# Hybrid decoder block on one core: squares of x one slot earlier, x fetched in two-k-tile rows on one queue, first slots multiplied by k-tile

## The chip, the core and the metric

The kernel runs on one NeuronCore of a Trainium2 chip. The metric is device time in microseconds (us), the median of three runs. Engines are named as the profile names them: PE is TensorE (PEld its weight loads), DVE is VectorE, ACT is ScalarE, POOL is GpSimd, SP is SyncE, which here issues most DMAs.

## What is computed

One decoder layer for 256 tokens and a model width of 1024, all in float32. Only the front of it matters here: an RMS norm whose result is multiplied by one wide weight matrix.

```python
n = rmsnorm(h, norm1_g[l])
z = n @ w_in[l]
cu, cg, q, k, v, gc, ga = jnp.split(z, cuts, axis=-1)
y_conv = conformer_conv(cu, cg, ...)
att = moba_attention(q, k, v, ...)
merged = sigmoid(gc) * y_conv + sigmoid(ga) * (att @ w_attn_out[l])
h = h + merged @ w_out[l]
h = h + swiglu(rmsnorm(h, norm2_g[l]), w_ffn_gate[l], w_ffn_up[l], w_ffn_down[l])
```

## The kernel before, in words

Every product is made of three float32r matmuls: each operand is split into a high part (rounded) and a low part (what the rounding left), and the product is high by high, low by high and high by low (L173 to L175 in `mm3`).

The weights come as a stream of **slots**. A slot is 512 KB: two k-tiles (128 rows of the matrix each) of 512 columns. For each slot a DMA fills a raw buffer (`stream_dma`, L137), ACT casts it to the high part `whi` (L154), DVE subtracts to get the low part `wlo` (L155; from slot 12 on POOL does every second one), and PE multiplies: 12 matmuls per slot, which are 2 token tiles by 2 k-tiles by 3. The first three slots are fetched and split in two pieces, one per k-tile. There are 5 raw buffers and 8 pairs of split buffers; the split runs 6 slots ahead of the multiplication. A slot's raw buffer is fetched anew when its low part has been made.

The first eight chunks of columns need `x`, transposed, as the stationary operand. `xT` holds the norm's gain in its first 16 columns and then eight k-tiles of 256 tokens. Five DMAs load it between the pieces of the first slots: k-tile 0 with the gain, k-tile 1, and then pairs (`load_x`, `between`). ACT makes the high part `xgh` (L698) and DVE the low part `xgl` (L699) of each k-tile, in `split_x`.

The norm's scale is not applied to `x`: the products are scaled when they leave PSUM. So the sum of squares is needed only after the first chunk (four slots). ACT squares `x` two k-tiles at a time (`square`, L709 and L712), POOL adds the four results up (three additions of 128x512, L713, and a last one of 128x256, L715), and four matmuls with one column (`ss`, L727, in `first_norm`) add up over the partitions. `first_norm` stands in `post[4]`, right behind slot 4 in PE's order. From `ss`, DVE and POOL make `rstd` (L728, L729), ACT's sigmoids `csg` (L318) and DVE's gating `ca` (L319) free the first chunk's PSUM banks and feed the convolution. That runs as 31 taps per channel tile on DVE (L271, L273), from transposed copies in PSUM that PE writes (`refill`, L261), while PE goes on with the slots.

The order of each engine's work is the order of the code. In a loop over six slots, before PE's loop, the code does the split of a slot, `split_x` of the next two k-tiles and one `square`:

```python
for i in range(6):
    stream_split(i + 1)
    for k in (2 * i + 2, 2 * i + 3):
        if k < KD:
            split_x(k)
    if i >= 2:
        square(i - 2)
```

In PE's loop a slot is multiplied for token tile 0 (`mm3(c, slot, g, 0)`), then come the DMA and split of later slots and the jobs of that slot, then token tile 1. Ten bf16 matmuls on a tile of zeros (L211) stand ahead of slot 0.

Of the kernel before, what the change touches and what calls it, by code (L numbers as in the profile page):

```python
# [19 lines left out]
T = S // P  # L20
# [5 lines left out]
CW = 512  # L26
G = 2
# [60 lines left out]
def hybrid_block(ctx: ExitStack, tc: tile.TileContext, x, xT, par, w_in, w_co, w_ao, w_o, w_gu, w_dn, out):  # L88
    nc = tc.nc
# [10 lines left out]
    def bank(name, *shape):  # L100
        return ps.tile([P, *shape], F32, tag="tr", bufs=2, name=name)


    slots = []
# [15 lines left out]
    raw, hi, lo = {}, {}, {}  # L120
    at = {"dma": 0, "split": 0}

    def shape_of(i):
        return (U, P) if isinstance(slots[i][0], Cols) else (G, CW)

    def parts(i):
        return [slice(j, j + 1) for j in range(G)] if i < 3 else [slice(None)]

    def stream_dma(upto):
        while at["dma"] < min(upto, len(slots)):  # L130
            i = at["dma"]
            c, g = slots[i]
            raw[i] = wp.tile([P, *shape_of(i)], F32, tag="raw", bufs=RAW_BUFS, name=f"raw{i}")
            for part in parts(i):
                if i == 0:
                    load_x(part.start, part.stop)
                (nc.sync if i or part.start else nc.scalar).dma_start(raw[i][:, part, :], c.w[g][:, part, :])  # L137
                between(i, part)
            at["dma"] += 1

# [3 lines left out]
    def stream_split(upto):  # L144
        while at["split"] < min(upto, len(slots)):
            i = at["split"]
            hi[i] = wp.tile([P, *shape_of(i)], F32R, tag="whi", bufs=SPL_BUFS, name=f"whi{i}")
            lo[i] = wp.tile([P, *shape_of(i)], F32R, tag="wlo", bufs=SPL_BUFS, name=f"wlo{i}")
            r = raw.pop(i)
            eng = nc.gpsimd if on_pool(i) else nc.vector  # L150
            for part in parts(i):
                if i == 0:
                    split_x(part.start)
                nc.scalar.copy(hi[i][:, part, :], r[:, part, :])  # L154
                eng.tensor_sub(lo[i][:, part, :], r[:, part, :], hi[i][:, part, :].bitcast(F32))  # L155
            at["split"] += 1
# [5 lines left out]
            .rearrange("p (k s) -> p k s", s=S) for x in "hl"  # L162
        )

    def mm3(c, i, g, t, acc=None, cols=slice(0, CW), first=0, last=None):

        xh, xl = c.lhs()
        acc = c.acc[t] if acc is None else acc
        last = c.nk - 1 if last is None else last
        tok = slice(t * P, (t + 1) * P)  # L170
        for j in range(G):
            k = g * G + j
            nc.tensor.matmul(acc, xh[:, k, tok], hi[i][:, j, cols], start=(k == first), stop=False)  # L173
            nc.tensor.matmul(acc, xl[:, k, tok], hi[i][:, j, cols], start=False, stop=False)  # L174
            nc.tensor.matmul(acc, xh[:, k, tok], lo[i][:, j, cols], start=False, stop=(k == last))  # L175
# [3 lines left out]
    def mm_cols(c, i, g, units, slot):  # L179
        xh, xl = c.rhs()  # L180
        for u in units:
            n, k = c.order[g * U + u]
            c.seen[n] += 1
            first, last = c.seen[n] == 1, c.seen[n] == c.nk
            if first:
                tag = GU_BANKS[banks["n"] % len(GU_BANKS)]
                banks["n"] += 1
                c.acc[n] = ps.tile([P, S], F32, tag=tag, bufs=4 if tag == "mm" else 1, name=f"{c.name}{n}")
            acc = c.acc[n]
            nc.tensor.matmul(acc, hi[i][:, u, :], xh[:, k, :], start=first, stop=False)  # L190
            nc.tensor.matmul(acc, hi[i][:, u, :], xl[:, k, :], start=False, stop=False)  # L191
            nc.tensor.matmul(acc, lo[i][:, u, :], xh[:, k, :], start=False, stop=last)  # L192
            if last:
                c.done(slot, n, c.acc.pop(n))
# [453 lines left out]
    def store(b, t, acc, cols=slice(0, CW)):  # L648
        to = slice(b * CW + cols.start, b * CW + cols.stop)
        o = sm.tile([P, cols.stop - cols.start], F32, tag="u", name=f"o{b}{t}{cols.start}")  # L650
        nc.vector.scalar_tensor_tensor(o, acc, rstd2[:, t : t + 1], xs[:, t, to], op0=ALU.mult, op1=ALU.add)
        nc.sync.dma_start(out[t * P : (t + 1) * P, to], o)
# [29 lines left out]
    def xk(k0, k1):  # L682
        return xt[:, XG + k0 * S : XG + k1 * S].rearrange("p (k s) -> p k s", s=S)

    def load_x(k0, k1):
        cols = slice(XG + k0 * S if k0 else 0, XG + k1 * S)
        nc.sync.dma_start(xt[:, cols], xT[:, cols])

    def between(i, part):
        if i == 0:  # L690
            if part.stop == G:
                load_x(2, 4)
        elif i < KD // 2 - 1 and part.stop == G:
            load_x(2 * i + 2, 2 * i + 4)

    def split_x(k):
        g, one = xt[:, k : k + 1], slice(k, k + 1)
        nc.scalar.activation(xg[0][0][:, one, :], xk(k, k + 1), AF.Copy, scale=g)  # L698
        nc.vector.scalar_tensor_tensor(xg[0][1][:, one, :], xk(k, k + 1), g, xg[0][0][:, one, :].bitcast(F32),  # L699
                                       op0=ALU.mult, op1=ALU.subtract)  # L700
# [5 lines left out]
    def square(q):  # L706

        if q == 0:
            nc.scalar.activation(sq, xk(0, 2), AF.Square)  # L709
            return  # L710
        s = sm.tile([P, 2, S], F32, tag="u", name=f"xsq{q}")
        nc.scalar.activation(s, xk(2 * q, 2 * q + 2), AF.Square)  # L712
        nc.gpsimd.tensor_add(sq, sq, s)  # L713
        if q == KD // 2 - 1:
            nc.gpsimd.tensor_add(sq[:, 0, :], sq[:, 0, :], sq[:, 1, :])  # L715

    for i in range(6):
        stream_split(i + 1)
        for k in (2 * i + 2, 2 * i + 3):
            if k < KD:  # L720
                split_x(k)
        if i >= 2:
            square(i - 2)
    def first_norm():
        ss = bank("ss", T)
        for t in range(T):
            nc.tensor.matmul(ss[:, t : t + 1], sq[:, 0, t * P : (t + 1) * P], ones, start=True, stop=True)  # L727
        nc.vector.tensor_scalar(rstd, ss, 1.0 / D, EPS, op0=ALU.mult, op1=ALU.add)  # L728
        nc.gpsimd.tensor_tensor(rstd, rstd, mhalf[:, :T], op=ALU.pow)  # L729
        nc.gpsimd.tensor_scalar_mul(rhalf, rstd, 0.5)  # L730
        nc.gpsimd.tensor_scalar_mul(gqs, prm[:, C_QG : C_QG + 1], float(P) ** -0.5)
# [7 lines left out]
    n = len(slots)  # L739
    tail = 3  # L740
    split_k = KF - tail * G
    for slot, (c, g) in enumerate(slots):
        rows = isinstance(c, Chunk)
        for job in pre.pop(slot, ()):
            job()
        if not rows:
            mm_cols(c, slot, g, range(U // 2), slot)
        elif g == 0:
            c.acc = [ps.tile([P, CW], F32, tag="mm", bufs=4, name=f"{c.name}_{t}") for t in range(T)]
        if rows and slot < n - tail:  # L750
            mm3(c, slot, g, 0)
        stream_dma(slot + AHEAD + RAW_BUFS)
        stream_split(slot + AHEAD)
        for job in jobs.pop(slot, ()):
            job()
        if not rows:
            mm_cols(c, slot, g, range(U // 2, U), slot)
        elif slot < n - tail:
            mm3(c, slot, g, 1, last=split_k - 1 if c is slots[-1][0] else None)
            if slot == n - tail - 1:  # L760
                end = xs[:, 1, D - CW :]
                nc.vector.scalar_tensor_tensor(end, c.acc[1], rstd2[:, 1:2], end, op0=ALU.mult, op1=ALU.add)
            for job in post.pop(slot, ()):
                job()
        elif slot == n - 1:
            for i in range(tail):
                mm3(c, n - tail + i, g - tail + 1 + i, 0)
            store(1, 0, c.acc[0])
            for part in range(2):
                cols = slice(part * CW // 2, (part + 1) * CW // 2)  # L770
                end = bank(f"end{part}", CW // 2)
                for i in range(tail):
                    mm3(c, n - tail + i, g - tail + 1 + i, 1, end, cols, first=split_k)
                store(1, 1, end, cols)
        load["pe"] += SLOT + pe_side.get(slot, 0.0)
        load["dve"] = max(load["dve"], load["pe"] - SLOT) + (0.0 if on_pool(slot + AHEAD) else LOW_PART) + dve_side.get(slot, 0.0)
        for job in late.pop(slot, ()):
            job()
        run_taps(slot, load["pe"] + LAG)
        if rows and g == c.nk // G - 1:  # L780
            c.done(slot, c.acc)
# [56 lines left out]
```

## Time and profile before

| what | value |
|---|---|
| median of 3 runs | 440.75 us (440.18 to 441.38) |
| the profiled execution | 441.83 us |
| its span, first to last instruction | 440.0 us |
| mean granted TensorE clock in the span | 0.996 of full |
| PE busy | 433.4 us (98%) |
| DVE, ACT, POOL busy | 316.7, 247.8, 90.1 us |

The page gives busy time by engine and the chain of work that ended last. The trace behind it answers with timelines of an engine (start, duration, engine, line, operation, tiles, and in brackets the idle time before it and what ended that), with waits in total, and with windows. A timeline merges neighbouring instructions of one line into a row with a count. A matmul's duration in a row is longer than its distance to the next, since matmuls overlap: distances are read from the starts.

### The profile page before, as it was taken

The page shows a single profiled execution, that of the slowest core. Times are in us where ns is not written, and L with a number is a line of the kernel's source. Part 1 is how long each engine was busy: PE and PEld are TensorE (multiplying, and loading weights), DVE is VectorE, ACT ScalarE, POOL GpSimd, SP SyncE. Part 2 cuts the span into 40 slices and gives each one's busy share as a digit, 9 for nine tenths or more (in the row PEclk, how much of TensorE's full clock was granted, in tenths as well). Part 3 has the DMA queues.
Part 4 walks back from the last instruction along what each step waited for, and adds up shares of the span by engine and source line. Part 5 has one row for each costly group of instructions (what it writes and reads, how often), then busy time and mean ns, then how long its engine had stood idle before and what let it go on. Part 6 is the DMA issues. An engine that isn't in the chain of part 4 may idle for free.

```text
span 440.0 us, 6863 instructions
## 1 busy us (share of the span) xinstructions
PE 433.4 (98%) x2514; PEld 378.1 (86%) x2514; DVE 316.7 (72%) x558; ACT 247.8 (56%) x451; POOL 90.1 (20%) x74
## 2 busy tenths in 40 slices
PE   8899999999999999999999999999999999999996
PEld 4678888888888888888888899999999999888886
DVE  4989998998889799967759368666666666744501
ACT  6844466779998776558525267554444444533300
POOL 1615575643655424200000000000000000000000
PEclk9989999999999999999999999999999999999999
DMA  8975573556435435554745545555555555766101
GB/s 276 346 263 209 193 292 119 182 192 203 141 136 192 144 112 176 192 191 144 242 160 176 194 137 194 190 194 192 193 191 192 192 195 192 251 223 198 44 0 49
DMA packets 23346, 80.30 MB, mean 182 GB/s; under 512 B 2576, under 2 KB 3216, under 8 KB 23312
## 3 DMA queue, kind: packets, MB, share of 16 engines
q1 hardware_dynamic: 22752, 78.40, 52.7%
q10 hardware_dynamic: 560, 1.46, 0.9%
q8 instruction: 20, 0.33, 0.3%
q14 instruction: 14, 0.11, 0.1%
HBM read 78.80 MB, written 1.05 MB: 181 GB/s over the span
## 4 chain that ended last, share of the span: by engine, by line
PE 93%; ACT 2%; POOL 2%; DMA 1%; DVE 1%; SPq 0%; issue 0%
PE gu L191 9%; PE gu L192 9%; PE gu L190 9%; PE dn L174 4%; PE dn L175 4%; PE dn L173 4%; PE g L175 3%; PE g L173 3%; PE g L174 3%; PE conv L173 2%; PE conv L175 2%; PE conv L174 2%; PE k L175 2%; PE k L173 2%; PE v L175 2%; PE q L173 2%
## 5 line engine op out<-in xcount | busy, mean ns | idle before, releaser
L155 DVE TENSOR_TENSOR wlo<-raw,whi 128x1024 fp32r<-128x1024 f32 (+1 forms) x125 | 155.0, 1258 | 25.9 <-ACT whi L154 25.0
L154 ACT CAST whi<-raw 128x1024 fp32r<-128x1024 f32 (+1 forms) x149 | 150.4, 1033 | 36.7 <-PE dn L174 19.9
L190 PE MATMUL gu<-hh,whi 128*128 128x256 f32 x352 | 97.8, 278 | 0.0
L191 PE MATMUL gu<-hl,whi 128*128 128x256 f32 x352 | 97.6, 277 | 0.1
L192 PE MATMUL gu<-hh,wlo 128*128 128x256 f32 x352 | 97.4, 277 | 0.0
L273 DVE SCALAR_TENSOR_TENSOR cacc<-cv,prm,cacc 128x256 f32<-128x256 f32 x240 | 97.1, 474 | 0.2
L155 POOL TENSOR_TENSOR wlo<-raw,whi 128x1024 fp32r<-128x1024 f32 x24 | 60.7, 2536 | 50.4 <-ACT whi L154 45.5
L191 PEld LDWEIGHTS gu<-hl,whi 128*128 128x128 f32 x352 | 66.1, 188 | 0.4 <-DVE hl L571 0.3
L190 PEld LDWEIGHTS gu<-hh,whi 128*128 128x128 f32 x352 | 66.1, 188 | 0.3 <-ACT hh L570 0.2
L192 PEld LDWEIGHTS gu<-hh,wlo 128*128 128x128 f32 x352 | 66.2, 188 | 0.0
L175 PE MATMUL dn<-wlo,fh 128*128 128x512 f32 x82 | 31.9, 389 | 0.0
L174 PE MATMUL dn<-whi,fl 128*128 128x512 f32 x82 | 31.9, 389 | 0.0
L173 PE MATMUL dn<-whi,fh 128*128 128x512 f32 x82 | 31.9, 389 | 0.0
L173 PE MATMUL conv<-whi,xgh 128*128 128x512 f32 x64 | 26.3, 412 | 0.4 <-ACT whi L154 0.4
L173 PE MATMUL g<-whi,xgh 128*128 128x512 f32 x64 | 26.4, 412 | 0.0
L626 DVE TENSOR_TENSOR f<-gu,fs 128x256 f32<-128x256 f32 x22 | 9.2, 424 | 23.0 <-PE gu L192 23.0
L175 PE MATMUL conv<-wlo,xgh 128*128 128x512 f32 x64 | 25.7, 402 | 0.0
L174 PE MATMUL conv<-whi,xgl 128*128 128x512 f32 x64 | 25.7, 402 | 0.0
L175 PE MATMUL g<-wlo,xgh 128*128 128x512 f32 x64 | 25.1, 393 | 0.0
L174 PE MATMUL g<-whi,xgl 128*128 128x512 f32 x64 | 25.0, 390 | 0.0
L633 ACT CAST fh<-f 128x256 fp32r<-128x256 f32 x22 | 8.8, 406 | 26.8 <-DVE f L626 26.7
L622 ACT ACTIVATE fs<-fg 128x256 f32<-128x256 f32 x22 | 9.1, 417 | 25.4 <-DVE fg L618 25.4
(163 smaller groups left out, 747.6 us busy)
## 6 DMA issues: line engine op xcount, KB each, us to landing
raw<-in_w_in SPq DMA_DIRECT2D x53, 512.0 KB, 4.1
raw<-in_w_gu SPq DMA_DIRECT2D x44, 512.0 KB, 3.3
raw<-in_w_dn SPq DMA_DIRECT2D x22, 512.0 KB, 4.0
raw<-in_w_ao SPq DMA_DIRECT2D x8, 512.0 KB, 3.3
raw<-in_w_co SPq DMA_DIRECT2D x8, 512.0 KB, 3.3
raw<-in_w_o SPq DMA_DIRECT2D x8, 512.0 KB, 4.7
raw<-in_w_in SPq DMA_DIRECT2D x5, 256.0 KB, 5.6
xs<-in_x ACTq DMA_DIRECT2D x1, 1024.0 KB, 4.8
```

The source lines that it names most:

```text
L154: nc.scalar.copy(hi[i][:, part, :], r[:, part, :])
L155: eng.tensor_sub(lo[i][:, part, :], r[:, part, :], hi[i][:, part, :].bitcast(F32))
L173: nc.tensor.matmul(acc, xh[:, k, tok], hi[i][:, j, cols], start=(k == first), stop=False)
L174: nc.tensor.matmul(acc, xl[:, k, tok], hi[i][:, j, cols], start=False, stop=False)
L175: nc.tensor.matmul(acc, xh[:, k, tok], lo[i][:, j, cols], start=False, stop=(k == last))
L190: nc.tensor.matmul(acc, hi[i][:, u, :], xh[:, k, :], start=first, stop=False)
L191: nc.tensor.matmul(acc, hi[i][:, u, :], xl[:, k, :], start=False, stop=False)
L192: nc.tensor.matmul(acc, lo[i][:, u, :], xh[:, k, :], start=False, stop=last)
L273: nc.vector.scalar_tensor_tensor(cacc[j], src, w, cacc[j], op0=ALU.mult, op1=ALU.add)
L622: nc.scalar.activation(st["s"], st["g"], AF.Silu)
L626: nc.vector.tensor_mul(st["f"], acc, st["s"])
L633: nc.scalar.copy(ff[0][0][:, j, :], st["f"])
```

## The change

Four edits. The square of k-tiles 2q and 2q+1 stands in round q+1 of the loop over six slots, where it stood in round q+2. The k-tiles 0 and 1 of x come in one DMA of 128 rows of 528 elements, where there were two of 272 and 256. The first weight piece is issued by SP behind that DMA, where ACT issued it. In slots 0 and 1 PE multiplies both token tiles by the first k-tile, then both by the second, ahead of the slot's other work.

```diff
             for part in parts(i):
-                if i == 0:
-                    load_x(part.start, part.stop)
-                (nc.sync if i or part.start else nc.scalar).dma_start(raw[i][:, part, :], c.w[g][:, part, :])
+                if i == 0 and part.start == 0:
+                    load_x(0, 2)
+                nc.sync.dma_start(raw[i][:, part, :], c.w[g][:, part, :])
                 between(i, part)
...
-    def mm3(c, i, g, t, acc=None, cols=slice(0, CW), first=0, last=None):
+    def mm3(c, i, g, t, acc=None, cols=slice(0, CW), first=0, last=None, pieces=range(G)):
...
-        for j in range(G):
+        for j in pieces:
...
-        if i >= 2:
-            square(i - 2)
+        if 1 <= i < 5:
+            square(i - 1)
...
-        if rows and slot < n - tail:
+        if slot < 2:
+            for j in range(G):
+                for t in range(T):
+                    mm3(c, slot, g, t, pieces=(j,))
+        elif rows and slot < n - tail:
             mm3(c, slot, g, 0)
...
         elif slot < n - tail:
-            mm3(c, slot, g, 1, last=split_k - 1 if c is slots[-1][0] else None)
+            if slot >= 2:
+                mm3(c, slot, g, 1, last=split_k - 1 if c is slots[-1][0] else None)
```

ACT, from the split of slot 2 to that of slot 5 (`whi` the high part of a slot, `xgh` that of a k-tile of x, `sq` and `xsq` the squares). Before:

```order
L698 ACTIVATE xgh<-xt 128x256 x2
L154 CAST whi_170<-raw_134 128x512 x2
L698 ACTIVATE xgh<-xt 128x256 x2
L709 ACTIVATE sq_145<-xt 128x512
L154 CAST whi_181<-raw_138 128x1024
L712 ACTIVATE xsq_185<-xt 128x512
L154 CAST whi_188<-raw_140 128x1024
L712 ACTIVATE xsq_192<-xt 128x512
L154 CAST whi_195<-raw_142 128x1024
L712 ACTIVATE xsq_199<-xt 128x512
```

And with the change:

```order
L698 ACTIVATE xgh<-xt 128x256 x2
L709 ACTIVATE sq_144<-xt 128x512
L154 CAST whi_170<-raw_133 128x512 x2
L698 ACTIVATE xgh<-xt 128x256 x2
L712 ACTIVATE xsq_180<-xt 128x512
L154 CAST whi_183<-raw_137 128x1024
L712 ACTIVATE xsq_187<-xt 128x512
L154 CAST whi_190<-raw_139 128x1024
L712 ACTIVATE xsq_194<-xt 128x512
L154 CAST whi_198<-raw_141 128x1024
```

Each square has moved ahead of one cast: the first ahead of slot 2's two casts, the second ahead of slot 3's, the last ahead of slot 5's.

SP, the first DMAs of the program (`xt` is x transposed, `raw` a slot's buffer). Before, with one more weight piece of slot 0 on ACT's queue:

```order
L687 DMA xt<-in_xT 128x272
L687 DMA xt<-in_xT 128x256
L137 DMA raw_124<-in_w_in 128x512
L687 DMA xt<-in_xT 128x512
L137 DMA raw_130<-in_w_in 128x512 x2
L687 DMA xt<-in_xT 128x512
```

And with the change, with none on ACT's queue:

```order
L687 DMA xt<-in_xT 128x528
L137 DMA raw_124<-in_w_in 128x512 x2
L687 DMA xt<-in_xT 128x512
L137 DMA raw_129<-in_w_in 128x512 x2
L687 DMA xt<-in_xT 128x512
```

From the third DMA on, SP issues the same ones in the same order; one issue fewer stands in the whole program.

## Rows read from the trace of the kernel before

**Rows 1.** The page: the chain that ended last, by engine.

```profile
PE 93%; ACT 2%; POOL 2%; DMA 1%; DVE 1%; SPq 0%; issue 0%
```

**Rows 2.** Waits of PE, whole span, the longest: us in total, times, longest.

```profile
PE ss L727 <- POOL sq L715: 1.8, 1, 1.8
```

**Rows 3.** Timeline of PE, 4.5 to 27.2 us.

```profile
7.02 0.50 PE L173 MATMUL conv<-whi,xgh 128*128 128x512 f32 x1 [0.35 <-ACT whi L154]
...
15.35 0.39 PE L175 MATMUL conv<-wlo,xgh 128*128 128x512 f32 x1
...
20.11 0.39 PE L175 MATMUL conv<-wlo,xgh 128*128 128x512 f32 x1
22.31 0.60 PE L727 MATMUL ss<-ones,sq 128*128 128x1 f32 x4 [1.80 <-POOL sq L715]
22.77 0.48 PE L173 MATMUL conv<-whi,xgh 128*128 128x512 f32 x1
27.20 0.39 PE L173 MATMUL conv<-whi,xgh 128*128 128x512 f32 x1
```

**Rows 4.** Window: us, busy PE, PEld, DVE, ACT, POOL, granted clock, DMA share, GB/s.

```profile
23.40:26.70 3.30, 3.30 (x10) 2.53 (x9) 2.27 (x3) 0.21 (x1) 0.86 (x2) 0.50 0.86 290
```

**Rows 5.** The chain that ended last, 9 to 22 us: start, duration, what.

```profile
9.42 0.91 ACT xgh L698 x2
10.34 1.03 ACT whi L154 x2
11.37 0.87 ACT xgh L698 x2
12.23 0.52 ACT sq L709
12.75 0.94 ACT whi L154
13.69 0.54 ACT xsq L712
14.30 1.81 POOL sq L713
...
18.42 2.17 POOL sq L713
...
20.66 1.60 POOL sq L715
```

**Rows 6.** Timeline of DVE, in three short stretches between 13 and 20 us.

```profile
13.73 1.23 DVE L155 TENSOR_TENSOR wlo<-raw,whi 128x1024 fp32r<-128x1024 f32 x1 [0.72 <-ACT whi L154]
...
17.11 2.32 DVE L155 TENSOR_TENSOR wlo<-raw,whi 128x1024 fp32r<-128x1024 f32 x1
...
19.35 2.32 DVE L155 TENSOR_TENSOR wlo<-raw,whi 128x1024 fp32r<-128x1024 f32 x1
```

**Rows 7.** The load of k-tiles 4 and 5: its issue on SP, its time to landing.

```profile
3.53 0.52 SPq L687 DMA_DIRECT2D xt<-in_xT  x1
DMA to landing us min/median/max: 5.9/5.9/5.9
```

**Rows 8.** Window 4 to 6 us, columns as in rows 4.

```profile
4.00:6.00 2.00, 2.00 (x6) 0.81 (x5) 1.29 (x3) 1.43 (x3) 0.00 (x0) 1.00 0.99 308
```

**Rows 9.** Window from 50 us; timelines of DVE, POOL, ACT, PE before the second refill.

```profile
50.00:60.00 10.00, 10.00 (x46) 8.29 (x45) 10.00 (x22) 4.73 (x6) 4.88 (x3) 1.00 0.80 298
...
63.91 3.12 DVE L155 TENSOR_TENSOR wlo<-raw,whi 128x1024 fp32r<-128x1024 f32 x1
68.68 0.61 DVE L255 MEMSET cv<- 128x30 f32 x2
...
63.56 2.39 POOL L155 TENSOR_TENSOR wlo<-raw,whi 128x1024 fp32r<-128x1024 f32 x1 [1.22 <-ACT whi L154]
...
55.09 0.47 ACT L318 ACTIVATE csg<-conv,rstd 128x256 f32<-128x256 f32 x1 [0.89 <-PE conv L175]
...
71.21 0.38 PE L261 MATMUL cv<-ident,ca 128*128 128x128 f32 x2
```

## The prediction

> **What bounds the kernel now.** I read the chain of waits first: 93% of the span is PE [rows 1], so a gain has to come out of time in which PE stands still or runs slowly. PE's waits name one: `ss` waits 1.8 us for the last sum on POOL [rows 2]. PE's timeline shows where. The last matmul of slot 4 starts at 20.11, `ss` at 22.31, slot 5 at 22.77; slot 6 starts at 27.20, so slot 5 lasts 4.43 us [rows 3]. The granted clock of 3.3 us of it is 0.50 (1.2 GHz; full is 2.4) [rows 4]. At the full rate, matmuls stand 0.227 us apart (21 steps from 15.35 to 20.11), slot 4 ends at 20.34, a slot takes 2.72, and the half clock costs 4.43 - 2.72 = 1.71. Before the clock fell, PE had been idle for 1.80 us and had then done four one-column matmuls. So the sum of squares costs 22.77 - 20.34 - 0.46 = 1.97 us of waiting and 1.71 of half clock, 3.68 in all. After 27 us PE has no wait that the profile lists.
>
> Why `ss` is late: ACT's work from 9.42 on is one gapless row of casts and squares up to the second square, which ends at 14.23; then POOL adds from 14.30 to 22.25 [rows 5]. A POOL addition and a DVE subtraction do not run at the same time here. The `wlo` with no addition beside it takes 1.23 us, those among additions 2.32 [rows 6]; the one from 17.11 ends at 19.43, and the addition that was asked for at 18.42 ends at 20.59, 1.16 later; the next `wlo` ends at 21.67, 1.08 after that, and the last addition at 22.25, 0.58 after that [rows 5, 6]. They take turns: 1.16 (or 0.58) for an addition, 1.08 for a subtraction.
>
> **The squares, moved up.** No instruction is added. From 9.42, ACT now does: k-tiles 4 and 5 0.91, square 0.52, slot 2's casts 1.03, k-tiles 6 and 7 0.87, second square 0.54. That ends at 13.30 in place of 14.23, since slot 3's cast (0.94) is now behind it [rows 5]. POOL begins at 13.38. The turns: addition to 14.54; `wlo` of slot 3, whose cast ends at 14.24, to 15.62; addition to 16.78; `wlo` of slot 4 to 17.86; addition to 19.02; `wlo` of slot 5 to 20.10; last addition to 20.68. `ss` may start at 20.73, 1.58 before now.
>
> What pays for that: slot 3's cast comes 0.54 later and its `wlo` waits for an addition, so it ends at 15.62 where it ended at 14.96 [rows 6]. PE wants it with the third matmul of slot 3, at 15.35 now [rows 3]: a new wait of 0.3 us, or 0.6 if PE comes earlier. From 15.65, 22 more steps of 0.227 end slot 4 at 20.64. So PE reaches `ss` just as the sum is ready: the stall is cut in two, 0.3 to 0.6 at slot 3 and 0.1 at `ss`, and slot 5 starts at 20.73 + 0.46 = 21.19, 1.58 earlier.
>
> The Trainium skill's page "SBUF — State Buffer", section "Who interferes with whom", states that a DVE instruction with two SBUF inputs and a GpSimd instruction that reads SBUF exclude each other, the second waiting for the whole of the first. It speaks against this edit, because it puts an addition in front of a subtraction that PE needs at once; the rows above agree with it (2.32 us against 1.23).
>
> **The clock.** PE's longest idle time there becomes 0.6 us, apart from the 0.46 of `ss`; in slot 0 it was idle for 0.35 [rows 3] and more than once held up, and the clock stayed at full through the following slots. I take it that it does not fall: 1.71 us less.
>
> **The first slots by k-tile.** PE has 1 us of holes in slot 0, the largest before 7.02, when the second piece's cast comes [rows 3]. Six matmuls of the first piece fill it. What follows is bound by ACT's casts, so slots 1 to 3 begin only some 0.3 earlier, and slot 3 then waits for its `wlo`. I count 0, its cover being that wait; without the cover it would be 0.3.
>
> **x in one DMA, the first piece on SP.** Only the landing of k-tiles 4 and 5 at 3.53 + 5.9 = 9.43 counts, since ACT took them at once at 9.42 [rows 5, 7]. The 256 KB piece leaves ACT's queue for the front of SP's; the two x loads became one, so from the third DMA on SP issues at the same times. The bytes ahead of k-tiles 4 and 5 are the same. Bounds: at worst the piece's 262 kB are now moved alone, at 308 GB/s [rows 8], 0.85 late; at best everything comes sooner by the one issue that is gone, 0.52 [rows 7]. I take 0, as the DMA engines were already busy for 0.99 of that window. The Trainium skill's "DMA: Bandwidth & Descriptors", section "Issuing engines are not separate DMA queues", says that issuing from several engines saves only the sequencer's time; by that, 0 is right too, and the fourth rival below has nothing to live on. ACT's own issue (0.4) goes, ahead of a table load that has 1.5 us of idle time behind it: 0.
>
> **What is late next.** PE is 1.58 + 1.71 = 3.29 us earlier from slot 6 on. The second refill, at 71.21, needs DVE's clearing, which ends at 69.29 [rows 9]: a reserve of 1.92. DVE has no gap on the way there (10.00 of 10 us from 50 on [rows 9]), and it begins that block only some 0.4 earlier: now it ends slot 7's `wlo`, the one behind the last addition, at 22.25 + 1.08 = 23.33; then it ends slot 6's behind the last addition, at 21.76, and slot 7's some 1.13 later, at 22.89, and two more `wlo` and `rstd` stand before the block as they do now. With PE at 67.92 and DVE at 68.85, 0.93 would be lost. But one of DVE's subtractions took 3.12 us, because POOL's at 63.56 stood in front of it [rows 9], and POOL's comes through casts and a DMA from the sigmoid at 55.09, which PE releases: it moves by 3.3 us while DVE moves by 0.4, and is over before DVE asks. That gives 1.9 back, DVE is at 66.95, and nothing is lost.
>
> **The sum.** 441.83 - 1.58 - 1.71 = 438.54 for the profiled execution. The median of the runs is 1.08 lower and the fastest run 1.65, which is close to the 1.71 of the half clock: some runs may not have had it. A run without it would only gain 1.58, to 438.6; if all had it, the median would go to 437.5. I take 438.3. 0.3% (1.3 us) is about what a measurement of this kernel tells from no change; the limits are 439.43 and 442.07.
>
> **Rivals.**
> 1. DVE binds the second refill: POOL's subtractions fall in front of DVE's again. For it: in the trace such pairs met four times in the block, of which the row is the worst. Against: that one is undone by the shift. It costs 0.93: 439.3.
> 2. The half clock stays, because the two short waits and `ss` are enough. For it: one fall was seen after 1.80 us of idle time, and no row tells how little is enough. Against: the early holes did nothing. It costs 1.71: 440.0.
> 3. The two engines slow each other instead of taking turns, so slot 3's `wlo` takes 2.32 from 14.26 and ends at 16.6. PE then reaches `ss` at 21.6, 0.9 later: 439.2. The ends 1.08 and 1.16 apart speak against it.
> 4. The edit does nothing: with the piece in front of it on one queue, k-tiles 4 and 5 land 0.85 late and eat half of the 1.58, while the half clock stays: 440.75 - 0.73 = 440.0.
> 5. Slower: the new wait at slot 3 makes the clock fall there, and the wait at `ss` makes it fall again. Slot 3 and 4 at half rate take 1.7 more, PE reaches `ss` at 22.4 instead of 20.64, as late as now, and slot 5 is slow as now, but in every run. From 440.18 for a run without a fall, 1.7 + 0.2 more is 442.1. It decides if a wait of 0.6 us is enough for a fall; the 0.35 in slot 0 was not.
>
> **The numbers.** Forecast 0.64, rivals 1 and 3 together 0.14, rival 2 0.10, rival 4 0.08, rival 5 0.04. Range 437.0 to 440.3: below, the median with the whole 3.29 and 0.5 from the DMAs; above, rivals 2 and 4 with 0.3 to spare. Faster: the forecast, and 0.09 of rivals 1 and 3, which lie just below 439.43: 0.73. Same: the rest of these, rivals 2 and 4: 0.23. Slower: 0.04.
>
> **What would show it.** Right: POOL's first addition near 13.4, `ss` near 20.7 with a wait under 0.3, a row of PE waiting for `wlo` in slot 3, clock 1.00 from 21 to 27, slot 6 near 23.9, no wait of PE at the second refill near 67.9. Wrong: k-tiles 4 and 5 taken after 9.8; a window at 0.50 after slot 3 or slot 5; `cv` waiting for DVE's memset; POOL's additions running beside `wlo`.

## The result, and the profile after

Median 438.54 us (437.73 to 438.78, 5 executions) against 441.36 (440.18 to 441.48, 5) for the kernel before on the same chip: ratio 0.995, 95% interval 0.9931 to 0.9968. The profiled execution took 437.82 us with a span of 436.0, against 441.83 and 440.0.

The page's chain by engine, which answers to [rows 1]:

```profile
PE 95%; ACT 1%; DMA 1%; DVE 1%; SPq 1%; issue 0%
```

POOL's 2% are gone from it. PE's waits over the whole span, from slot 0 on, answer to [rows 2] (us in total, times, longest):

```profile
PE conv L175 <- DVE wlo L155: 0.4, 1, 0.4
PE conv L173 <- ACT whi L154: 0.2, 1, 0.2
```

`ss` no longer waits; a low part in slot 3 does. PE's timeline shows both, beside [rows 3]:

```profile
15.33 0.50 PE L175 MATMUL conv<-wlo,xgh 128*128 128x512 f32 x1 [0.37 <-DVE wlo L155]
...
20.23 0.39 PE L175 MATMUL conv<-wlo,xgh 128*128 128x512 f32 x1
20.45 0.56 PE L727 MATMUL ss<-ones,sq 128*128 128x1 f32 x4
20.87 0.48 PE L173 MATMUL conv<-whi,xgh 128*128 128x512 f32 x1
...
23.72 0.39 PE L173 MATMUL conv<-whi,xgh 128*128 128x512 f32 x1
```

Slot 5 starts at 20.87, 1.90 earlier, and lasts 23.72 - 20.87 = 2.85 where it lasted 4.43. Slot 6 starts 3.48 earlier. The window of slot 5, columns as in [rows 4], shows the full clock:

```profile
20.50:23.70 3.20, 3.20 (x17) 2.71 (x17) 3.20 (x4) 1.15 (x2) 0.00 (x0) 1.00 0.79 245
```

The chain of waits ahead of that, against [rows 5] (start, duration, what), has lost POOL. It goes from ACT through a low part on DVE to slot 3:

```profile
3.52 5.43 DMA xt<-in_xT
8.98 0.91 ACT xgh L698 x2
9.89 0.52 ACT sq L709
10.41 1.03 ACT whi L154 x2
11.44 0.81 ACT xgh L698 x2
12.25 0.52 ACT xsq L712
12.77 0.95 ACT whi L154
13.74 1.54 DVE wlo L155
15.33 0.50 PE conv L175
```

POOL's timeline, and DVE's, against [rows 6], show the turns:

```profile
12.86 1.34 POOL L713 TENSOR_TENSOR sq<-sq,xsq 128x512 f32<-128x512 f32 x1 [10.35 <-ACT xsq L712]
14.39 4.27 POOL L713 TENSOR_TENSOR sq<-sq,xsq 128x512 f32<-128x512 f32 x2 [0.20 <-ACT xsq L712]
18.74 1.61 POOL L715 TENSOR_TENSOR sq<-sq 128x256 f32<-128x256 f32 x1
...
13.74 1.53 DVE L155 TENSOR_TENSOR wlo<-raw,whi 128x1024 fp32r<-128x1024 f32 x1 [0.71 <-ACT whi L154]
17.43 2.31 DVE L155 TENSOR_TENSOR wlo<-raw,whi 128x1024 fp32r<-128x1024 f32 x1
```

The first addition ends at 14.20 and slot 3's `wlo`, asked for at 13.74, ends 1.07 later, at 15.27; the last addition ends at 20.35. Before the second refill, against [rows 9] (DVE, POOL, PE):

```profile
63.62 1.35 DVE L155 TENSOR_TENSOR wlo<-raw,whi 128x1024 fp32r<-128x1024 f32 x1
66.62 0.61 DVE L255 MEMSET cv<- 128x30 f32 x2
...
61.48 2.40 POOL L155 TENSOR_TENSOR wlo<-raw,whi 128x1024 fp32r<-128x1024 f32 x1 [2.80 <-ACT whi L154]
...
67.71 0.60 PE L261 MATMUL cv<-ident,ca 128*128 128x128 f32 x4
```

The subtraction of 3.12 us takes 1.35, DVE's clearing ends at 67.23, PE comes at 67.71 and does not wait. The span is 4.0 us shorter, which is more than 3.48. From slot 6 on, the two executions are alike except in one stretch of `gu` matmuls, those of the gate and up products late in the layer (windows with the columns of [rows 4], before and after):

```profile
256.40:268.60 12.20, 12.20 (x107) 12.20 (x106) 8.46 (x14) 8.04 (x15) 0.90 (x2) 1.00 0.32 102
252.90:264.70 11.80, 11.80 (x107) 11.80 (x106) 8.15 (x14) 8.06 (x15) 0.90 (x2) 1.00 0.32 97
```

These 0.4 us are not the change's. Counted from the starts of the same 107 matmuls, the stretch takes 12.53 us before and 12.52 or 12.53 in `no_sq`, `x_one`, `no_adds` and `cand3` below, and 12.12 or 12.13 in the change and in the eight other profiles, among them `fill` and `w_sp`, which keep the squares where they were. What decides it is open.

### The profile page after: what moved, and what is told of

It reads as the page before. It is cut to its first block, busy times and chain, and to the rows that moved or that the text cites. A ratio compares the mean times of both kernels' runs of the same rounds, so it can differ in the third digit from the quotient of the medians.

```text
span 436.0 us, 6861 instructions
## 1 busy us (share of the span) xinstructions
PE 431.2 (99%) x2514; PEld 376.4 (86%) x2514; DVE 314.8 (72%) x558; ACT 248.1 (57%) x451; POOL 87.3 (20%) x74
## 4 chain that ended last, share of the span: by engine, by line
PE 95%; ACT 1%; DMA 1%; DVE 1%; SPq 1%; issue 0%
PE gu L191 9%; PE gu L192 9%; PE gu L190 9%; PE dn L174 4%; PE dn L175 4%; PE dn L173 4%; PE g L175 3%; PE g L173 3%; PE g L174 3%; PE conv L175 3%; PE conv L173 3%; PE conv L174 3%; PE k L175 2%; PE k L173 2%; PE q L175 2%; PE v L175 2%
## 5 line engine op out<-in xcount | busy, mean ns | idle before, releaser
L155 DVE TENSOR_TENSOR wlo<-raw,whi 128x1024 fp32r<-128x1024 f32 (+1 forms) x125 | 153.4, 1245 | 25.3 <-ACT whi L154 24.5
L155 POOL TENSOR_TENSOR wlo<-raw,whi 128x1024 fp32r<-128x1024 f32 x24 | 59.3, 2473 | 51.1 <-ACT whi L154 46.2
```

## The experiments

**Two groups of executions.** Medians hide something that nearly every comparison below needs. The mean granted clock is known for each execution. Beside the experiments, 63 executions of the kernel before were timed: 29 had 0.999 or 1.0 and took 439.3 to 440.5 us, and 34 had 0.995 or 0.996 and took 441.0 to 442.0. So a clock fall like that of [rows 4] comes in about half of its executions, and those take 1.6 us more. Where in the program the clock fell is known for the profiled execution alone; for the others it is taken from the mean clock, 0.996 as there.

**The squares alone** (`sq_only`): the kernel before with

```diff
-        if i >= 2:
-            square(i - 2)
+        if 1 <= i < 5:
+            square(i - 1)
```

> The kernel before with the squares moved up and nothing else. Theory (the sum of squares is late by a row of ACT work and by turns of POOL and DVE, and the wait brings the half clock): the row starts at 9.42 us as before, POOL's first addition near 13.4, ss near 20.8 without a long wait, clock 1.00 from 21 to 27, about 3.2 us less than before. Rival 1 (the first slots by k-tile or the DMAs bring the gain): less than 1 us. Rival 2 (the half clock comes from something else than the wait): 1.5 us.

Measured: 438.4 us, ratio 0.9952, interval 0.9933 to 0.997; no execution with a fall. Slot 5 starts at 21.20 and slot 6 at 24.07, with no wait at `ss`:

```profile
20.81 0.53 PE L727 MATMUL ss<-ones,sq 128*128 128x1 f32 x4
...
24.07 0.39 PE L173 MATMUL conv<-whi,xgh 128*128 128x512 f32 x1
```

This edit carries the whole gain.

**All but the squares** (`no_sq`): the change with that edit put back.

```diff
-        if 1 <= i < 5:
-            square(i - 1)
+        if i >= 2:
+            square(i - 2)
```

> The changed kernel with the squares put back. Theory: k-tiles 4 and 5 are taken at 8.98 as in the changed kernel, the sum comes 0.4 earlier than before, PE gets to it earlier and waits 2 us or more, the half clock is back; 0.4 us less than before, about 3 us more than the changed kernel. Rival 1 (k-tile order or DMAs bring the gain): 2 to 3 us less than before.

Measured: 440.65 us, ratio 1.0004, interval 0.9988 to 1.002. Six executions without a fall have a median of 439.90, six with it 441.33. The profiled one had none. PE's longest wait in it:

```profile
PE ss L727 <- POOL sq L715: 1.9, 1, 1.9
```

The window of slot 5, columns as in [rows 4]:

```profile
22.50:25.40 2.90, 2.90 (x14) 2.39 (x14) 2.90 (x4) 0.00 (x0) 0.00 (x0) 1.00 0.77 283
```

So PE was idle for 1.92 us ahead of `ss`, more than the 1.80 of [rows 3], and its clock stayed at full. The other edits are worth nothing that can be measured.

**The change without its DMA edit** (`no_dma`): x in two loads, the first piece on ACT again.

```diff
-                if i == 0 and part.start == 0:
-                    load_x(0, 2)
-                nc.sync.dma_start(raw[i][:, part, :], c.w[g][:, part, :])
+                if i == 0:
+                    load_x(part.start, part.stop)
+                (nc.sync if i or part.start else nc.scalar).dma_start(raw[i][:, part, :], c.w[g][:, part, :])
```

> The changed kernel with its loads as before: x in two DMAs, the first weight piece on ACT's queue. Theory: everything from the casts of k-tiles 4 and 5 on comes 0.45 later than in the changed kernel, so 0.45 us more than that and 3 us less than before. Rival (the loads do nothing, the row of ACT work makes it up): as the changed kernel.

Measured: 438.3 us, ratio 0.9946, interval 0.993 to 0.9963; k-tiles 4 and 5 taken by ACT at 9.26, slot 5 at 21.15.

**The change without the k-tile order** (`no_kt`):

```diff
-        if slot < 2:
-            for j in range(G):
-                for t in range(T):
-                    mm3(c, slot, g, t, pieces=(j,))
-        elif rows and slot < n - tail:
+        if rows and slot < n - tail:
             mm3(c, slot, g, 0)
...
-            if slot >= 2:
-                mm3(c, slot, g, 1, last=split_k - 1 if c is slots[-1][0] else None)
+            mm3(c, slot, g, 1, last=split_k - 1 if c is slots[-1][0] else None)
```

> The changed kernel with token tile by token tile in slots 0 and 1. Theory: PE comes later out of slot 1 by up to 0.5 us, and the wait for slot 3's low part takes that up; as the changed kernel within 0.2 us, with no or a shorter wait in slot 3. Rival 1 (the k-tile order brings part of the gain): 0.5 to 1 us more than the changed kernel.

Measured: 438.33 us, ratio 0.995, interval 0.9932 to 0.9968, span 436.0, the same as the change. PE waits 0.7 us in slot 0 and no more in slot 3; slot 5 starts at 20.84. The order moves a wait.

**The kernel before with PE kept busy** (`fill`): nine matmuls on zeros ahead of `ss`.

```diff
     def first_norm():
+        for _ in range(9):
+            nc.tensor.matmul(wps, warm, warm[:, None, :].to_broadcast([P, 4, P]), start=True, stop=True)
         ss = bank("ss", T)
```

> The kernel before with nine bf16 matmuls on the tile of zeros in front of ss, which fill the time in which PE waits for the sum. They add work and move nothing else. Theory (the idle time makes the clock fall): ss at 22.3 to 22.5 as before, clock 1.00 from 23 to 27, slot 5 takes 2.72 in place of 4.43 us, 1.7 us less at slot 6; at the end 1.3 to 1.7 less, the rest lost if DVE binds the second refill. Rival (the fall has another cause): half clock as before, the time as before or up to 0.3 more.

Measured: 439.98 us, ratio 0.9987, interval 0.9974 to 1.0. Eleven of twelve executions had no fall (median 439.96) and one had it (441.41); the kernel before beside it had 9 without (439.97) and 8 with it (441.48). PE's timeline:

```profile
20.63 2.12 PE L726 MATMUL wps<-warm 128*128 128x512 bf16 x9
22.58 0.50 PE L729 MATMUL ss<-ones,sq 128*128 128x1 f32 x4
22.94 0.48 PE L173 MATMUL conv<-whi,xgh 128*128 128x512 f32 x1
...
25.79 0.39 PE L173 MATMUL conv<-whi,xgh 128*128 128x512 f32 x1
```

With the stall filled and slot 5 as late as before, the fall becomes rare and the executions without it are no faster. Waiting and fall are two separate costs.

**The change without three of POOL's additions** (`no_adds`). It leaves the sums out: the first norm then takes its sum of squares from two of the eight k-tiles.

```diff
         nc.scalar.activation(s, xk(2 * q, 2 * q + 2), AF.Square)
-        nc.gpsimd.tensor_add(sq, sq, s)
```

> The changed kernel without POOL's three additions of 128x512, so that the norm's sum has only two of the eight k-tiles of x. Theory (POOL and DVE take turns): every subtraction of 128x1024 from slot 3 on takes 1.23 us, PE's wait in slot 3 is under 0.2, slot 5 starts 0.4 to 0.5 earlier than in the changed kernel, the end 0.4 to 0.6 earlier. Rival (the long subtractions come from the DMA traffic of that stretch): they stay near 2.3 us and the time stays.

Measured: 437.83 us, ratio 0.9936, interval 0.9916 to 0.9956; slot 5 at 20.62. DVE's timeline:

```profile
13.86 1.23 DVE L155 TENSOR_TENSOR wlo<-raw,whi 128x1024 fp32r<-128x1024 f32 x1 [0.56 <-ACT whi L154]
15.33 1.23 DVE L155 TENSOR_TENSOR wlo<-raw,whi 128x1024 fp32r<-128x1024 f32 x1 [0.24 <-ACT whi L154]
16.81 4.63 DVE L155 TENSOR_TENSOR wlo<-raw,whi 128x1024 fp32r<-128x1024 f32 x4 [0.25 <-ACT whi L154]
```

Without an addition every subtraction is back at 1.23 (the row of four holds 4.63, with starts 1.13 to 1.14 apart). Slot 5 starts 0.25 us before that of the change (20.87), although ACT took k-tiles 4 and 5 later, at 9.10 against 8.98. Counted from there, slot 5 starts 11.52 us on, and 11.89 in the change: 0.37 us is what the change still pays for the turns.

**x in one load alone** (`x_one`, one execution) and **the first piece on SP alone** (`w_sp`, one execution), each on the kernel before:

```diff
# x_one
-                if i == 0:
-                    load_x(part.start, part.stop)
+                if i == 0 and part.start == 0:
+                    load_x(0, 2)
# w_sp
-                (nc.sync if i or part.start else nc.scalar).dma_start(raw[i][:, part, :], c.w[g][:, part, :])
+                nc.sync.dma_start(raw[i][:, part, :], c.w[g][:, part, :])
```

> The kernel before with the first two k-tiles of x in one DMA, the first weight piece still on ACT's queue. If the larger rows or the one issue less bring the earlier landing, k-tiles 4 and 5 are taken near 8.98; if the single queue does, at 9.42. The end: 0.4 less than before, or as before.

> The kernel before with the first weight piece issued by SP behind the first k-tile of x, which is still loaded in two DMAs. If the single queue brings the earlier landing, k-tiles 4 and 5 are taken near 8.98; if the larger rows or the one issue less do, at 9.42 or later, since SP now has one issue more ahead of them (0.47).

Measured: 439.49 us at clock 1.0, and 440.55 at 0.996. SP issues k-tiles 4 and 5 at 3.06 and at 4.01, and they land at 8.62 and at 9.94. PE's longest wait with x in one load:

```profile
PE ss L727 <- POOL sq L715: 1.6, 1, 1.6
```

With the first piece on SP, PE's timeline in slot 0:

```profile
8.04 0.69 PE L173 MATMUL conv<-whi,xgh 128*128 128x512 f32 x1 [1.66 <-ACT whi L154]
```

The window behind that wait, columns as in [rows 4]:

```profile
8.20:11.60 3.40, 3.40 (x9) 2.50 (x10) 3.40 (x8) 3.40 (x8) 0.00 (x0) 0.50 1.05 390
```

With x in one load, SP has one issue fewer ahead of k-tiles 4 and 5, and they land 0.8 us sooner than in [rows 7]; with the first piece on SP it has one more, and they land 0.5 later. Each is one execution. The one load also has longer rows, and no run tests these alone; the change has them with as many issues ahead as before. In the change the two halves of the edit nearly cancel. The fall can also come in slot 0, after 1.66 us of idle time. There it took the place of the later stall: PE came late enough to wait only 0.05 us at `ss`, and slot 5 started at 23.37.

**One load for x with the first piece on ACT** (`cand1`), on top of the change:

```diff
-                nc.sync.dma_start(raw[i][:, part, :], c.w[g][:, part, :])
+                (nc.sync if i or part.start else nc.scalar).dma_start(raw[i][:, part, :], c.w[g][:, part, :])
```

> The changed kernel with x in one DMA instead of two, the first piece of the weight kept on ACT's queue; the squares stay one slot up and the first slots by k-tile. With one SP issue less ahead of the load of k-tiles 4 and 5 than in the changed kernel, that load should land near 8.6 us, as it did with x in one DMA before (8.62), against 9.0 on average in the changed kernel. Theory A, the start of the second piece's work sets everything behind it: ACT and POOL start about 0.35 us sooner, slot 5 starts near 20.5 to 20.6, no half clock, and the time is 0.3 us below the changed kernel, near 438.1 where that gives 438.4. Theory B, TensorE's own matmuls and the low parts of slot 3 set slot 5's start: the landing moves and slot 5 stays near 20.87, no difference. Ratio to before 0.994 by A, 0.995 by B.

Measured: 437.52 us, ratio 0.9935, interval 0.9914 to 0.9955, which overlaps that of the change. k-tiles 4 and 5 are taken at 8.86, slot 5 starts at 20.74, and PE's wait in slot 3 has grown:

```profile
PE conv L175 <- DVE wlo L155: 0.6, 1, 0.6
```

k-tiles 4 and 5 are taken 0.12 us before those of the change, and slot 5 starts 0.13 before: it follows them, as theory A has it, but they came at 8.86 and not near 8.6. PE comes 0.34 sooner to slot 3, the low part 0.12, and PE waits 0.22 longer for it. The time is lower than either theory gave, and these starts do not explain that.

**That, with the low parts of slot 3 last and the norm behind the first token tile of slot 5** (`cand2`):

```diff
+        if slot == 5:
+            mm3(c, slot, g, 0)
+            first_norm()
...
+        elif slot == 3:
+            for which in "hl":
+                for t in range(T):
+                    mm3(c, slot, g, t, last=-1 if which == "h" else None, which=which)
```

> As the run with x in one DMA, and two orders on TensorE: in slot 3 the eight matmuls with the high part first and the low parts behind them, and the norm's sum of eight k-tiles behind the first token tile of slot 5 instead of ahead of it. Theory A, the wait in slot 3 (0.37 us in the changed kernel) is the last early one: it goes, slot 5 starts 0.4 us sooner than in the run with x in one DMA, and the time is 0.7 us below the changed kernel, 437.6 where that gives 438.4. Theory B, VectorE's refill binds next: the reserve of its clear at the second refill was 0.48 us in the changed kernel, so a gain of 0.8 us ahead of it comes back as a wait of 0.3 us there, and the time is 437.9. Theory C, the wait only moves to the low parts at the slot's end: the time is that of the run with x in one DMA.

Measured: 437.21 us, ratio 0.9929, interval 0.9905 to 0.9953; `cand1` beside it has 437.52, and the intervals overlap. The first refill comes at 27.00, where it was at 27.69 in the kernel without these two orders: the wait in slot 3 is gone. But of the six executions four took 436.9 to 437.4 and two 438.2 and 438.4. The profiled one is the 438.2; PE, DVE and POOL in it:

```profile
67.69 0.96 PE L263 MATMUL cv<-ident,ca 128*128 128x128 f32 x4 [0.60 <-DVE cv L257]
...
41.72 3.18 DVE L155 TENSOR_TENSOR wlo<-raw,whi 128x1024 fp32r<-128x1024 f32 x1
...
41.41 2.41 POOL L155 TENSOR_TENSOR wlo<-raw,whi 128x1024 fp32r<-128x1024 f32 x1 [4.61 <-DVE cacc L275]
```

POOL's subtraction starts 0.31 us before DVE's, and DVE's takes 3.18. In the kernel without the two orders POOL's stood at 42.08, and DVE's came first:

```profile
41.68 1.21 DVE L155 TENSOR_TENSOR wlo<-raw,whi 128x1024 fp32r<-128x1024 f32 x1
```

In both, POOL starts 0.07 to 0.08 us behind the end of a cast on ACT (41.33 here, 42.01 there), though the bracket of POOL's row names DVE; the cast has come forward by as much as PE at the first refill. DVE is then late for the second refill and PE waits 0.60, where theory B gave 0.3. This is the mechanism of the prediction's first rival, in another kernel. That it makes the two groups is not shown: no execution of the lower group was profiled.

**That, with slot 14's low part on POOL** (`cand3`), and **the change once more** (`after_2`) beside it:

```diff
-            eng = nc.gpsimd if on_pool(i) else nc.vector
+            eng = nc.gpsimd if on_pool(i) or i == 14 else nc.vector
```

> The run with x in one DMA and both orders on TensorE, and one low part more on POOL (that of slot 14, which VectorE made in 3.18 us behind one of POOL's). In that run the profiled execution waited 0.60 us for VectorE at the second refill and was 0.5 us behind the run without the two orders there, although it was 0.69 us ahead at the first refill; of its six executions four took 436.9 to 437.4 and two 438.2 to 438.4. Theory A, the meeting of the two engines at slot 14 is what loses the gain in some executions: without it VectorE is 2 to 3 us earlier, no wait at the second refill, and all executions are near 437.0. Theory B, the two groups have another cause: both groups stay.

> The changed kernel once more, beside the run above on the same chip: 438.4 and ratio 0.995 to before, as the first time; no execution with the half clock (granted clock 0.999 or 1.0 in each). The run above should be 1.3 us below it by its theory A; if the first landing is as late as in the earliest profiles, k-tiles 4 and 5 are taken at 9.0 here.

Measured: 437.03 us (436.85 to 437.66, 6 executions), ratio 0.9914, interval 0.9896 to 0.9931, against 438.28, ratio 0.9952, interval 0.9934 to 0.997, for the change. The second refill, DVE's clearing before it and POOL's three subtractions in a row:

```profile
67.14 0.60 PE L263 MATMUL cv<-ident,ca 128*128 128x128 f32 x4
...
65.34 0.61 DVE L257 MEMSET cv<- 128x30 f32 x2
...
30.75 7.15 POOL L155 TENSOR_TENSOR wlo<-raw,whi 128x1024 fp32r<-128x1024 f32 x3 [4.84 <-ACT whi L154]
```

The clearing ends 1.2 us ahead of PE, and 2.2 before that of `cand2`, as theory A gave. But the long meeting is not gone. It has moved to the next subtraction that DVE makes beside one of POOL's:

```profile
44.33 3.14 DVE L155 TENSOR_TENSOR wlo<-raw,whi 128x1024 fp32r<-128x1024 f32 x1
```

The reserve comes from DVE having one subtraction fewer on the way. The upper group of `cand2` is not seen, though six executions are few: if one in three still belonged to it, none of six would come by chance about one time in eleven. All six executions lie below all twelve of the change (437.98 and up): this version beats both kernels.

The change's own repeat holds its times but for one execution, 442.41 us at a clock of 0.996. Here slot 5 starts at 21.17 and POOL's last addition ends at 20.65. The single fall was not in the profiled execution, so its place is not known.

## Why the prediction was right

**The squares: right in its mechanism.** The turns came as worked out, about 0.35 us earlier. Slot 3's `wlo` was put at 15.62 and ended at 15.27; the last addition was put at 20.68 and ended at 20.35; each end between them lies 0.35 or 0.36 early. The new wait at slot 3 (0.3 to 0.6) was 0.37 as idle time and 0.53 by the starts (14.57 to 15.33, less a step of 0.227), and `ss` had none where 0.1 was given.

How near slot 5's start came to 21.19 is partly luck. In the six profiles with the squares moved, the additions in place and PE's order from slot 3 on as in the change (the change, `after_2`, `no_dma`, `no_kt`, `sq_only`, `cand1`), it stands 11.88 to 11.90 us behind ACT's taking of k-tiles 4 and 5. The prediction's terms give 21.19 - 9.42 = 11.77. Most of the 0.12 is the first addition, which was counted at 1.16 us and took 1.34. In `no_dma` and `after_2` slot 5 starts at 21.15 and 21.17, because ACT took the k-tiles 0.15 before 9.42, which about makes up for that.

**The DMAs: counted 0, and not settled within its bounds.** The 0.35 is what is left, after the longer first addition, of k-tiles 4 and 5 being taken at 8.98 and not at 9.42, although SP issued them at 3.52 as against 3.53. Nor was it right that only their landing counts. ACT came to them without a gap from k-tiles 2 and 3, for which it had waited, and the difference stood there already (before, and after):

```profile
7.47 0.91 ACT L698 ACTIVATE xgh<-xt 128x256 fp32r<-128x256 f32 x2 [0.50 <-DMA xt<-in_xT]
7.01 0.91 ACT L698 ACTIVATE xgh<-xt 128x256 fp32r<-128x256 f32 x2 [1.25 <-DMA xt<-in_xT]
```

In the repeat ACT took k-tiles 4 and 5 at 9.27. Over the profiles, kernels with the loads as before took them at 9.42, 9.32, 9.26 and 9.22, and kernels with the change's loads at 8.98, 9.16, 8.95, 9.10 and 9.27. The means are 9.31 and 9.09, a difference of 0.2 inside a scatter of 0.3; the timed runs with and without the edit, 438.3 to 438.5, don't tell them apart. The reason given for 0, that the DMA engines were busy, did not hold for its parts, which moved the landing by -0.8 and +0.5.

**The half clock: the mechanism right, the size off.** The term of 1.71 went as said, but slot 5 at the full rate takes 2.85, not 2.72, so it was worth 4.43 - 2.85 = 1.58. And it applies to about half of the executions of before. The remark that some executions may not have had it was the right reading of a median that lay 1.08 below the profiled time. An execution without the fall gains about 1.5 (439.8 against 438.3), one with it 3.1.

**The k-tile order: 0, right**, with its cover as named: without it the wait stands in slot 0, and with it in slot 3. The size was off: slots 1, 2 and 3 began 0.98, 0.55 and 0.55 us earlier than before, and not some 0.3, but the wait in slot 3 took that up.

**The second refill: no wait, right, on a thinner margin.** PE was put at 67.92 and DVE at 66.95, a reserve of 0.97; they came at 67.71 and 67.23, a reserve of 0.48. The step that was mis-sized is "that gives 1.9 back". The 3.12 did shrink to 1.35, but DVE's other meetings with POOL changed as well: the four subtractions that had taken 1.55, 1.97, 1.59 and 3.12, in all 8.23, took 2.08, 1.87, 1.87 and 1.35, in all 7.17, which gives 1.06 back. The first of the four, before and after:

```profile
36.77 1.55 DVE L155 TENSOR_TENSOR wlo<-raw,whi 128x1024 fp32r<-128x1024 f32 x1
35.77 2.08 DVE L155 TENSOR_TENSOR wlo<-raw,whi 128x1024 fp32r<-128x1024 f32 x1
```

Nor was POOL's subtraction over before DVE asked: it moved by 2.08 us, from 63.56 to 61.48, and not by 3.3, and ended 0.26 after DVE's had started at 63.62. DVE also began the block sooner than was said: this first one stands at 35.77 where it stood at 36.77, 1.0 earlier and not 0.4. This 1.0 and the 1.06 make up the 2.06 by which the clearing moved.

**The sum.** 438.54 was given for the profiled execution and 438.3 for the median; they were 437.82 and 438.54, and 438.28 for the median of the repeat. At slot 6 the profiled execution is 3.48 earlier where 3.29 was given, out of two errors against each other: 1.90 and not 1.58 for the start of slot 5, 1.58 and not 1.71 for the clock. Another 0.4 of its 0.72 is the stretch of `gu`, which no term had. The 438.3 was a choice between 438.6 and 437.5 and not a sum. That it is so near is in part luck.

**The rivals.** DVE did not bind the refill in the change; in the profiled execution of `cand2`, with PE 0.7 us earlier, it did. The half clock did not stay. The engines took turns and did not slow each other: slot 3's `wlo` ended at 15.27, 1.07 behind the addition, and not at 16.6. The edit did something. The slower case, a fall at the short waits, was not seen in 16 of the change's 17 executions; the 442.41 of the other is close to the 442.1 it gave, but whether it is that mechanism stays open.

## What to carry to other kernels

A stall on the critical engine may cost twice, once as waiting and once as a clock that falls behind it; look at the granted clock of several executions before summing, since the second cost may come in only some of them. When two engines share turns, moving one instruction forward moves every later meeting: count all of them, not only the worst. And a gain that depends on another engine's reserve may appear in some executions and not in others; here it stayed in all six once DVE had one subtraction fewer, though six are few.

## What was not expected of the hardware

- In these profiles the length of the idle time alone does not decide the clock's fall: 1.80 and 1.66 us were followed by a clock of 0.50, while 1.92 was not. And executions of the kernel before come with a fall and without one, 34 to 29.
- SP issues DMAs 0.47 us apart at the start. With one issue more ahead of the load of k-tiles 4 and 5, it landed 0.5 us later, and with one issue fewer and longer rows 0.8 sooner, although the same bytes were asked for ahead of it and the DMA engines were busy in the kernel before (0.99 of the window in [rows 8]). The three later kernels with x in one load and the first piece on ACT agree: ACT took these k-tiles at 8.86, 8.40 and 8.56.
- A few tenths decide a meeting of two engines: where POOL's subtraction started 0.31 us ahead of DVE's, DVE's took 3.18 us; where it started 0.40 behind, 1.21.
